# Two weight sums on VectorE, an earlier first chunk, and plain products moved between the MLP's loops

## The chip, the core and the metric

The kernel runs on one core of a Trainium2 chip. The metric is the device time of one execution in microseconds (us); a time is given as the median of several executions. The engines are TensorE (PE, matmul, with its weight load PEld), VectorE (DVE), ScalarE (ACT), GpSimd (POOL) and SyncE (SP, which here only issues DMAs). GpSimd's queue issues DMAs too, the accumulating ones.

## The reference

A decoder trunk of two layers on 1024 tokens of 1024 features, in float32. Layer 0 mixes tokens with multi-head latent attention (MLA), layer 1 with stick-breaking attention. Each is followed by cross-attention into 256 memory tokens and an MLP with squared ReLU:

```python
for i in range(DEPTH):
    a = rmsnorm(h, norm_mix[i])
    h = h + (mla_mixer(...) if i % 2 == 0 else stick_breaking_mixer(...))
    h = h + mem_cross_attn(rmsnorm(h, norm_cross[i]), rmsnorm(mem, norm_mem[i]), ...)
    h = h + jnp.square(jax.nn.relu(rmsnorm(h, norm_mlp[i]) @ w_in)) @ w_out   # 1024 -> 4096 -> 1024
return rmsnorm(h, norm_final)
```

## The kernel before

**Tiles.** Activations lie transposed: `x[c][f]` is a 128x512 tile of features f (8 of them) and tokens of chunk c (2 chunks of 512). A product in float32 is made of three fast matmuls (`mm3`, L103 to L105): each operand is split into a high half, a cast by ScalarE (L98, L159), and a low half, what the cast left over, a subtraction by GpSimd or VectorE (L90). Tiles come from pools by tag; a tag has a fixed number of slots (`p` 6, `w` 8, `a` 32, `g` 24, `o` 8, `f` 4, `raw` 3, `tmp` 5; in PSUM `s` 3 and `acc` 3), and a new tile waits until the oldest of its tag is free. A scheduler fixes the order of the instructions on each engine from a model of their costs.

**Sublayers.** `mla` and `stick` interleave projections and attention through `weave`, and `weave` also steps a side job, `aside[0]`, in two of three turns. `cross` ends with output units `ounit(c, m)` of 12 matmuls, each added to `x[c][m]` by `add_x` (L256). After the last feature of a chunk, `ready` finishes the RMS norm of the chunk, writes 8 normed tiles (`normed`, L212) into tiles `p` and splits them into `a` tiles for the MLP.

**MLP.** Of 4096 hidden features 3584 go through a scheme of seven products in place of eight (`seven`): two token chunks, two halves of the input and two halves of the output form 2x2 blocks. On the activation side it needs B11, B21, B22 and sums T1 to T4, on the weight side A11, A12, A22 and sums S1 to S4, where S2 = S1 + A11 and S4 = S2 + A12. `win` (14 per layer, 84 matmuls each) makes hidden tiles, squares them and spills seven of them to DRAM (L1054); `wout` (17 per layer) fetches them (`fetch`, L1069) and adds into `x`. The other 512 hidden features are "plain": 8 products of 24 matmuls before the first `win`, squared by VectorE (L991) and spilled, and 16 output products of 12 matmuls (192 matmuls) at the end of the MLP. In between `quad(k)` makes the T sums, for which VectorE computes the normed tiles again (L212) and then four sums (L879).

**Weight sums.** The side job `weight_sums` forms S1 to S4 in DRAM while the attention runs: `begin` copies one block on SP's queue (L924), `add` adds another by an accumulating DMA on GpSimd's queue (L929). There are 12 blocks per sum (`S1_out31` is a block of S1 for `w_out`, group 3, half 1). A `win` then loads three A and four S blocks of weights, a `wout` likewise (L1086).

**Ends.** After layer 0's MLP the last output products feed layer 1's norm (`stagger`, `ready`); after layer 1's they go through `finish`, which norms and writes the output.

## Time and profile before

| | us |
|---|---|
| median of 3 executions | 2764.06 (2758.38 to 2767.03) |
| the profiled execution, its own time | 2767.62 |
| its span in the trace | 2765.8 |
| TensorE busy in the span | 2574.7 |
| VectorE busy | 1640.6 |
| ScalarE busy | 1298.1 |
| GpSimd busy | 1389.3 |

The trace is of one execution. The page gives totals and groups of instructions; the answers of the trace used here are of four kinds: busy time of each engine by stretch, a timeline of single instructions, groups by line of code, and DMA issues. In a timeline the bracket at the end of a row says how long the engine stood idle before that instruction, and which instruction, or DMA, released it. The stages by time: MLA to about 500 us, cross-attention to 669, layer 0's MLP to about 1350 (`win` from 745, `wout` from 1027), stick-breaking and cross-attention to about 2060, layer 1's MLP to the end.

### The profile page before, as it was taken

Reading aid. Unit: us, or ns where it says so; the run is one execution under the profiler, and the core shown is the slowest. Engines: PE = TensorE matmul, PEld = TensorE weight load, DVE = VectorE, ACT = ScalarE, POOL = GpSimd, SP = SyncE. Lnnn points to the kernel's source line nnn. Section 1 sums busy time; section 2 is a strip of 40 time slices with the busy share of each in tenths; the row PEclk is TensorE's granted clock in tenths of the full one; section 3 lists DMA queues with packets and bytes.
Section 4 is the critical chain, followed back from the end, with each engine's and each line's share of the span. In section 5 each row is a group of like instructions: output and inputs, shape, how many; then the busy total and the mean of one; then the engine's idle time right before and its main releaser. Section 6 shows DMA issues by size and latency. Waiting matters only on the chain.

```text
span 2765.8 us, 37140 instructions
## 1 busy us (share of the span) xinstructions
PE 2574.7 (93%) x12774; PEld 2138.5 (77%) x12774; DVE 1640.6 (59%) x2754; ACT 1298.1 (47%) x2558; POOL 1389.3 (50%) x1098
## 2 busy tenths in 40 slices
PE   7897988898899989999999899989998999899997
PEld 5786877786688867888888787877776888678886
DVE  6765766666834436445655757587669343364457
ACT  6674755553345445443443333344543545454432
POOL 4443454633744439665432333436337544397653
PEclk9998999999899999999999999999999999999998
DMA  3528594510366648663251827855102655486632
GB/s 117 194 78 220 119 215 123 132 35 27 103 185 198 186 161 261 197 193 100 82 174 63 212 69 153 194 131 129 35 23 85 197 188 189 147 273 193 195 107 76
DMA packets 204206, 398.34 MB, mean 144 GB/s; under 512 B 23025, under 2 KB 77297, under 8 KB 190705
## 3 DMA queue, kind: packets, MB, share of 16 engines
q1 hardware_dynamic: 191584, 337.11, 38.8%
q0 software_dynamic: 12288, 58.73, 11.2%
q8 instruction: 100, 1.64, 0.2%
q14 instruction: 90, 0.73, 0.1%
q10 hardware_dynamic: 144, 0.13, 0.0%
HBM read 336.11 MB, written 177.21 MB: 186 GB/s over the span
## 4 chain that ended last, share of the span: by engine, by line
PE 64%; DVE 13%; DMA 4%; issue 2%; POOL 2%; ACT 2%; SPq 0%; DVEq 0%; POOLq 0%; ACTq 0%
PE ps_acc L103 13%; PE ps_acc L104 13%; PE ps_acc L105 13%; PE ps_s L103 7%; PE ps_s L104 7%; PE ps_s L105 7%; DVE p L212 2%; DVE f L462 2%; PE ps_s L398 1%; DVE p L879 1%; DVE x L256 1%; DVE p L467 1%; POOL w L90 1%; PE ps_pt L420 1%; DMA raw<-in_w_xv 1%
## 5 line engine op out<-in xcount | busy, mean ns | idle before, releaser
L90 POOL TENSOR_TENSOR w<-raw,w 128x512 fp32r<-128x512 f32 (+3 forms) x313 | 415.1, 1341 | 478.0 <-ACT w L98 338.5
L90 POOL TENSOR_TENSOR g<-tmp,g 128x512 fp32r<-128x512 f32 x176 | 238.1, 1354 | 278.5 <-ACT g L193 211.1
L103 PE MATMUL ps_acc<-a,w 128*128 128x512 f32 (+1 forms) x820 | 319.4, 390 | 14.0 <-ACT a L159 4.2
L104 PE MATMUL ps_acc<-a,w 128*128 128x512 f32 (+1 forms) x820 | 316.6, 387 | 3.8 <-DVE a L201 2.0
L105 PE MATMUL ps_acc<-a,w 128*128 128x512 f32 (+1 forms) x820 | 316.8, 386 | 2.3 <-POOL w L90 2.3
L256 DVE TENSOR_TENSOR x<-ps_acc,x 128x512 f32<-128x512 f32 x296 | 200.1, 684 | 104.8 <-PE ps_acc L105 103.0
L98 ACT CAST w<-raw 128x512 fp32r<-128x512 f32 (+2 forms) x189 | 114.2, 605 | 238.3 <-PE ps_acc L104 149.8
L103 PE MATMUL ps_s<-a,w 128*128 128x512 f32 (+1 forms) x416 | 169.1, 406 | 37.7 <-ACT a L159 21.5
L103 PEld LDWEIGHTS ps_acc<-a,w 128*128 128x128 f32 x820 | 156.5, 191 | 47.0 <-ACT a L159 4.7
L90 POOL TENSOR_TENSOR a<-p,a 128x512 fp32r<-128x512 f32 x100 | 137.0, 1375 | 102.7 <-ACT a L159 81.9
L104 PEld LDWEIGHTS ps_acc<-a,w 128*128 128x128 f32 x820 | 156.3, 191 | 36.5 <-DVE a L201 4.2
L105 PEld LDWEIGHTS ps_acc<-a,w 128*128 128x128 f32 x820 | 156.0, 190 | 33.8 <-POOL w L90 3.5
L398 PE MATMUL ps_s<-g 128*128 128x512 f32 (+3 forms) x576 | 141.1, 359 | 36.0 <-POOL g L90 29.5
L104 PE MATMUL ps_s<-a,w 128*128 128x512 f32 (+1 forms) x416 | 168.6, 405 | 5.5 <-POOL a L90 2.3
L105 PE MATMUL ps_s<-a,w 128*128 128x512 f32 (+1 forms) x416 | 166.9, 402 | 4.5 <-POOL w L90 4.5
L90 DVE TENSOR_TENSOR a<-tmp,a 128x512 fp32r<-128x512 f32 x92 | 90.9, 993 | 134.2 <-ACT a L159 133.3
L90 DVE TENSOR_TENSOR pt<-ps_pt,pt 128x512 fp32r<-128x512 f32 (+1 forms) x192 | 122.2, 639 | 67.8 <-ACT pt L176 67.1
L176 ACT CAST pt<-ps_pt 128x512 fp32r<-128x512 f32 (+1 forms) x192 | 104.9, 554 | 87.8 <-PE ps_pt L420 46.0
L103 PE MATMUL ps_acc<-o,w 128*128 128x512 f32 x304 | 129.1, 425 | 11.5 <-DVE x L256 8.5
L398 PEld LDWEIGHTS ps_s<-g 128*128 128x128 f32 x576 | 95.6, 192 | 51.3 <-POOL g L90 30.7
L159 ACT CAST a<-tmp 128x512 fp32r<-128x512 f32 x100 | 62.1, 621 | 148.6 <-DMA tmp<-B 139.1
L159 ACT CAST a<-p 128x512 fp32r<-128x512 f32 x116 | 72.0, 620 | 116.7 <-PE ps_s L104 43.0
(313 smaller groups left out, 7569.3 us busy)
## 6 DMA issues: line engine op xcount, KB each, us to landing
p<-S_in SPq DMA_DIRECT2D x112, 256.0 KB, 3.0
tmp<-T SPq DMA_DIRECT2D x112, 256.0 KB, 3.4
raw<-in_w_in SPq DMA_DIRECT2D x100, 256.0 KB, 2.9
S_in<-in_w_in POOLq DMA_DIRECT2D x24, 1024.0 KB, 10.8
S_out<-in_w_out POOLq DMA_DIRECT2D x48, 512.0 KB, 9.3
tmp<-B SPq DMA_DIRECT2D x84, 256.0 KB, 3.2
T<-tmp SPq DMA_DIRECT2D x56, 256.0 KB, 3.1
S_in<-in_w_in SPq DMA_DIRECT2D x12, 1024.0 KB, 8.9
```

What stands on the lines that cost most here:

```text
L90: eng.tensor_tensor(out=l, in0=full, in1=h.bitcast(F32), op=ALU.subtract)
L98: nc.scalar.copy(out=h, in_=raw)
L103: nc.tensor.matmul(out=ps, lhsT=wh, rhs=xh, start=start, stop=False, skip_group_check=True)
L104: nc.tensor.matmul(out=ps, lhsT=wh, rhs=xl, start=False, stop=False, skip_group_check=True)
L105: nc.tensor.matmul(out=ps, lhsT=wl, rhs=xh, start=False, stop=stop, skip_group_check=True)
L159: nc.scalar.copy(out=h, in_=src)
L176: nc.scalar.copy(out=h, in_=ps)
L212: nc.vector.scalar_tensor_tensor(out=t, in0=x[c][f], scalar=gains[:, gcol + f:gcol + f + 1], in1=rms[c][1], op0=ALU.mult, op1=ALU.mult)
L256: nc.vector.tensor_tensor(out=x[c][f], in0=ps, in1=x[c][f], op=ALU.add)
L398: nc.tensor.matmul(out=ps[:, :n], lhsT=lh, rhs=rh, start=(i == 0), stop=(i == len(passes) - 1), skip_group_check=True)
L420: nc.tensor.transpose(out=tp[:, o0:o0 + P], in_=col(probs[qi][kb // 4], kb % 4), identity=ident)
L462: nc.vector.tensor_tensor_scan(out=rev, data0=rev, data1=pt[j][:, :n], op0=ALU.mult, op1=ALU.bypass, initial=1.0 if j == len(pieces) - 1 e ...
```

## The change

1. Only S1 and S3 are formed in DRAM; the side job is stepped in one of three turns. S2 and S4 are formed by VectorE in `seven_weights`, S4 in the tile of S2, in each `win` and `wout`.
2. In `cross` all remaining output units of chunk 0 go before those of chunk 1.
3. `ready` keeps the normed tiles (tags `g` for chunk 0, `o` and `p` for chunk 1), and `quad` uses them in place. The plain input products run chunk 0 first, then chunk 1 with a `quad` before each. Their squares go to ScalarE. One T4 split in two goes to VectorE.
4. Of the plain output products' 4 hidden tiles, 2 (layer 0) or 1 (layer 1) are multiplied early, between the last `win` and the first `wout`: their operands are loaded and split during the last `win`. Each `x` tile takes one more addition for it. The rest stays at the end.

GpSimd in MLA, before: the S1 adds (L929) and the subtractions of low halves (L90; `g` for attention scores, `w` for weights).

```order
L929 DMA S1_out10_0_1306<-in_w_out 32x2x2048
L929 DMA S1_out11_0_1369<-in_w_out 32x2x2048
L929 DMA S1_in20_0_1390<-in_w_in 32x4x2048
L90 TENSOR_TENSOR g_2561<-tmp_2559,g_2560 128x512
L929 DMA S1_out20_0_1431<-in_w_out 32x2x2048
L929 DMA S1_out21_0_1463<-in_w_out 32x2x2048
L90 TENSOR_TENSOR w_2794<-raw_2791,w_2793 128x512
L90 TENSOR_TENSOR g_2663<-tmp_2661,g_2662 128x512
L929 DMA S1_in30_0_1522<-in_w_in 32x2x2048
L929 DMA S1_out30_0_1542<-in_w_out 128x2x256
L929 DMA S1_out31_0_1576<-in_w_out 128x2x256
```

And now, the end of the same sum:

```order
L90 TENSOR_TENSOR g_4310<-tmp_4308,g_4309 128x512
L929 DMA S1_in30_0_2006<-in_w_in 32x2x2048
L90 TENSOR_TENSOR g_4424<-tmp_4422,g_4423 128x512
L929 DMA S1_out30_0_2131<-in_w_out 128x2x256
L90 TENSOR_TENSOR w_4580<-raw_4577,w_4579 128x512
L90 TENSOR_TENSOR g_4469<-tmp_4467,g_4468 128x512
L929 DMA S1_out31_0_2210<-in_w_out 128x2x256
L90 TENSOR_TENSOR w_4586<-raw_4583,w_4585 128x512
L90 TENSOR_TENSOR w_4614<-raw_4611,w_4613 128x256
L90 TENSOR_TENSOR g_4552<-tmp_4550,g_4551 128x512
L90 TENSOR_TENSOR w_4620<-raw_4617,w_4619 128x384
```

The last adds of S1 stand apart, with subtractions between them. S2's adds and copies are not in the program any more.

VectorE at the entry of layer 0's MLP, before: normed tiles again (L212), T sums (L879) and squares (L991).

```order
L879 TENSOR_TENSOR p<-p 128x512
L212 SCALAR_TENSOR_TENSOR p<-x,gains,tmp 128x512
L879 TENSOR_TENSOR p<-p 128x512 x4
L212 SCALAR_TENSOR_TENSOR p<-x,gains,tmp 128x512 x2
L879 TENSOR_TENSOR p<-p 128x512
L991 TENSOR_TENSOR pt<-pt 128x512 x2
L879 TENSOR_TENSOR p<-p 128x512
L212 SCALAR_TENSOR_TENSOR p<-x,gains,tmp 128x512
L879 TENSOR_TENSOR p<-p 128x512
L212 SCALAR_TENSOR_TENSOR p<-x,gains,tmp 128x512 x2
L991 TENSOR_TENSOR pt<-pt 128x512
```

And now, from chunk 1's normed tiles on (`g` are chunk 0's kept tiles, `o` and `p` chunk 1's):

```order
L212 SCALAR_TENSOR_TENSOR o<-x,gains,tmp 128x512 x3
L212 SCALAR_TENSOR_TENSOR p<-x,gains,tmp 128x512
L212 SCALAR_TENSOR_TENSOR o<-x,gains,tmp 128x512 x3
L212 SCALAR_TENSOR_TENSOR p<-x,gains,tmp 128x512
L879 TENSOR_TENSOR g<-g,o 128x512 x3
L90 TENSOR_TENSOR a<-o,a 128x512
L879 TENSOR_TENSOR g<-g,p 128x512
L90 TENSOR_TENSOR a<-p,a 128x512
L90 TENSOR_TENSOR a<-o,a 128x512
L879 TENSOR_TENSOR o<-o 128x512
L90 TENSOR_TENSOR a<-p,a 128x512
L879 TENSOR_TENSOR o<-o 128x512 x2
```

The second computation of the normed tiles and the squares are gone from VectorE; splits of chunk 1 (L90) stand among the sums.

TensorE from the last `win` (`ps_acc<-a,a`) to the first `wout` (`ps_s<-a,w`) of layer 0, before:

```order
L105 MATMUL ps_acc_10218<-a_7576,a_10209 128x512
L103 MATMUL ps_acc_10218<-a_7582,a_10208 128x512
L104 MATMUL ps_acc_10218<-a_7583,a_10208 128x512
L105 MATMUL ps_acc_10218<-a_7582,a_10209 128x512
L103 MATMUL ps_s_10422<-a_10340,w_10382 128x512
L104 MATMUL ps_s_10422<-a_10341,w_10382 128x512
L105 MATMUL ps_s_10422<-a_10340,w_10383 128x512
L103 MATMUL ps_s_10423<-g_10346,w_10388 128x512
```

Now, at the end of the last `win`, where early plain products (`ps_acc_10266`) follow:

```order
L105 MATMUL ps_acc_10100<-a_7504,a_10091 128x512
L103 MATMUL ps_acc_10100<-a_7510,a_10090 128x512
L104 MATMUL ps_acc_10100<-a_7511,a_10090 128x512
L105 MATMUL ps_acc_10100<-a_7510,a_10091 128x512
L104 MATMUL ps_acc_10266<-a_10163,w_10142 128x512
L105 MATMUL ps_acc_10266<-a_10162,w_10143 128x512
L103 MATMUL ps_acc_10266<-a_10168,w_10142 128x512
L104 MATMUL ps_acc_10266<-a_10169,w_10142 128x512
```

and 71 matmuls behind that last `win` product, the first `wout` (`ps_s_10483`):

```order
L105 MATMUL ps_s_10384<-a_10116,w_10365 128x512
L103 MATMUL ps_s_10384<-a_10122,w_10364 128x512
L104 MATMUL ps_s_10384<-a_10123,w_10364 128x512
L105 MATMUL ps_s_10384<-a_10122,w_10365 128x512
L103 MATMUL ps_s_10483<-a_10402,w_10447 128x512
L104 MATMUL ps_s_10483<-a_10403,w_10447 128x512
L105 MATMUL ps_s_10483<-a_10402,w_10448 128x512
L103 MATMUL ps_acc_10392<-a_10162,w_10364 128x512
```

The early plain products (96 matmuls in layer 0, some of them ahead of the last `win`'s end) fill the place where the two loops met.

The diff, cut to its core:

```diff
@@ ready
-                    t = T("p")
+                    t = T("g" if c == 0 else "o" if k % 4 < 3 else "p")
                     normed(t, c, k, gcol)
-                    act[c].append(split(t, "a", nc.vector if k % 2 else nc.gpsimd))
+                    act[c].append((t, *split(t, "a", nc.vector if k % 2 else nc.gpsimd)))
@@ weave
-            if turn[0] % 3 < 2:
+            if turn[0] % 3 == 0:
                 next(aside[0], None)
@@ cross
+        for m in range(4, FT):
+            run(ounit(0, m))
         for m in range(FT):
-            if m + 4 < FT:
-                run(ounit(0, m + 4))
             run(ounit(1, m))
@@ weight_sums
         yield from add("S1", 1, 1)
-        yield from begin("S2", other("S1"))
         yield from add("S3", 1, 0)
-        yield from add("S2", 0, 0)
-        yield from begin("S4", other("S2"))
-        yield from add("S4", 0, 1)
+
+    def seven_weights(load, n, stage, tags):
...
+        a11, s1, s2 = load("A11", "raw"), load("S1", stage), T(stage)[:, :n * P]
+        take_split("A11", a11)
+        tt(nc.vector, s2, s1, a11, ALU.add)
+        take_split("S2", s2)
+        a12 = load("A12", "raw")
+        take_split("A12", a12)
+        tt(nc.vector, s2, s2, a12, ALU.add)
+        take_split("S3", load("S3", stage))
+        take_split("S1", s1)
+        take_split("A22", load("A22", "raw"))
+        take_split("S4", s2)
+        return r
@@ mlp
         def quad(k):
-            b11, b12, b22, b21 = (T("p") for _ in range(4))
-            for t, c, f in ((b11, 0, k), (b12, 1, k), (b22, 1, k + 4), (b21, 0, k + 4)):
-                normed(t, c, f, gcol)
+            b11, b12, b22, b21 = n0[k][0], n1[k][0], n1[k + 4][0], n0[k + 4][0]
...
+            b["T4"].append(split(b21, "o", ve if k % 2 else po))
+            b["T2"].append(split(b22, "g", po))
...
+        for c, ac in enumerate((a0, a1)):
+            for f in range(nk):
+                if c == 0:
+                    ws.append([load_w(ins["w_in"][i, f, j], "wwfp"[f]) for j in range(2)])
+                else:
+                    quad(f)
...
-                nc.vector.tensor_tensor(out=t, in0=t, in1=t, op=ALU.mult)
+                nc.scalar.activation(out=t, in_=t, func=AF.Square)
...
+        early, late = (range(2), range(2, nk)) if gnext is not None else (range(1), range(1, nk))
...
         for n, kp in enumerate(pairs):
-            win(n, kp)
+            win(n, kp, aside if kp == pairs[-1] else ())
+        for m in range(0, FT, 2):
+            if len(wp) <= m // 2:
+                block()
+            wh, wl = wp[m // 2]
+            for j in range(2):
+                for c in range(NC_):
+                    ps = PS("acc" if c else "s")
+                    project([(col(wh, j, ne * P), col(wl, j, ne * P))], ne, [g[c, k] for k in early], ps)
+                    add_x(c, m + j, ps)
...
-            project([w], nk, [g[c, k] for k in range(nk)], ps)
+            project([w], nl, [g[c, k] for k in late], ps)
```

## Rows read from the trace of the kernel before

**Rows 1.** the page's part 1: engine, busy time (share of the span), instructions

```profile
PE 2574.7 (93%) x12774; PEld 2138.5 (77%) x12774; DVE 1640.6 (59%) x2754; ACT 1298.1 (47%) x2558; POOL 1389.3 (50%) x1098
```

**Rows 2.** busy us by stretch: engines (instructions), granted clock, DMA share, GB/s

```profile
core 0: us, PE busy (x) PEld busy (x) DVE busy (x) ACT busy (x) POOL busy (x), PEclk, DMA share, GB/s
655.00:762.00 107.00, 87.04 (x333) 66.43 (x333) 87.15 (x104) 42.33 (x73) 73.64 (x48) 0.87 0.26 83
762.00:1010.00 248.00, 248.00 (x1074) 201.50 (x1073) 93.80 (x115) 121.00 (x203) 113.29 (x86) 1.00 0.58 180
1010.00:1060.00 50.00, 38.77 (x148) 28.51 (x147) 28.64 (x35) 27.67 (x56) 32.50 (x30) 0.90 0.76 245
1060.00:1300.00 240.00, 238.39 (x1031) 193.12 (x1030) 116.08 (x145) 98.53 (x176) 166.80 (x132) 1.00 0.61 181
1300.00:1352.00 52.00, 52.00 (x229) 42.36 (x229) 38.03 (x49) 25.86 (x45) 31.74 (x25) 1.00 0.22 65
2045.00:2155.00 110.00, 90.32 (x349) 68.68 (x348) 88.25 (x104) 44.38 (x76) 75.42 (x49) 0.89 0.28 89
2400.00:2450.00 50.00, 37.94 (x147) 27.88 (x146) 29.42 (x35) 26.82 (x55) 32.33 (x30) 0.90 0.74 244
2690.00:2766.00 76.00, 55.37 (x337) 48.65 (x335) 61.62 (x134) 18.14 (x37) 26.34 (x20) 0.88 0.23 78
```

**Rows 3.** timeline of TensorE in MLA: start, length, instruction, [idle before, releaser]

```profile
258.94 0.80 PE L398 MATMUL ps_s<-g 128*128 128x512 f32 x1 [15.35 <-POOL g L90]
...
420.38 0.80 PE L398 MATMUL ps_s<-g 128*128 128x512 f32 x1 [10.86 <-POOL g L90]
```

**Rows 4.** timeline of GpSimd in MLA, the two adds before those waits

```profile
254.29 1.15 POOL L929 DMA_DIRECT2D S_out<-in_w_out  x1 [12.76 <-DMA S_out<-S_out]
...
415.99 1.16 POOL L929 DMA_DIRECT2D S_out<-in_w_out  x1 [17.03 <-DMA S_in<-S_in]
```

**Rows 5.** DMA issues, 210 to 260 us: count, KB each, us to landing

```profile
S_out<-in_w_out POOLq DMA_DIRECT2D x5, 512.0 KB, 18.7
```

**Rows 6.** the page's DMA issues, whole program, same columns

```profile
S_out<-in_w_out POOLq DMA_DIRECT2D x48, 512.0 KB, 9.3
```

**Rows 7.** timeline of VectorE at the first MLP's entry, first and last

```profile
669.87 6.10 DVE L212 SCALAR_TENSOR_TENSOR p<-x,gains,tmp 128x512 f32<-128x512 f32 x6 [0.76 <-ACT tmp L115]
...
741.80 1.75 DVE L879 TENSOR_TENSOR p<-p 128x512 f32<-128x512 f32 x1
```

**Rows 8.** timelines of TensorE and of SP from last win to first wout

```profile
1018.49 0.39 PE L105 MATMUL ps_acc<-a 128*128 128x512 f32 x1
1027.45 0.80 PE L103 MATMUL ps_s<-a,w 128*128 128x512 f32 x1 [8.57 <-ACT a L159]
...
1023.77 0.45 SPq L1069 DMA_DIRECT2D tmp<-B  x1
```

**Rows 9.** VectorE's groups, 655 to 762 us: busy us, mean ns, idle

```profile
L212 DVE SCALAR_TENSOR_TENSOR p<-x,gains,tmp 128x512 f32<-128x512 f32 x32 | 37.0, 1192 | 1.1 <-ACT tmp L115 1.1
L879 DVE TENSOR_TENSOR p<-p 128x512 f32<-128x512 f32 x16 | 20.2, 1270 | 0.1
L991 DVE TENSOR_TENSOR pt<-pt 128x512 f32<-128x512 f32 x8 | 9.4, 1186 | 6.1 <-ACT pt L990 6.1
```

**Rows 10.** GpSimd's groups, 655 to 762 us, same columns

```profile
L90 POOL TENSOR_TENSOR g<-p,g 128x512 fp32r<-128x512 f32 x12 | 21.8, 1829 | 7.6 <-ACT g L159 7.6
L90 POOL TENSOR_TENSOR a<-p,a 128x512 fp32r<-128x512 f32 x13 | 19.9, 1544 | 14.6 <-ACT a L159 14.6
```

**Rows 11.** VectorE's groups of the whole program, each shape apart

```profile
L256 DVE TENSOR_TENSOR x<-ps_acc,x 128x512 f32<-128x512 f32 x296 | 200.1, 684 | 104.8 <-PE ps_acc L105 103.0
```

**Rows 12.** timeline of VectorE, one addition without and one beside GpSimd

```profile
1005.80 0.69 DVE L879 TENSOR_TENSOR f<-tmp,pt 128x512 f32<-128x512 f32 x1 [0.77 <-ACT pt L1016]
...
716.40 1.77 DVE L879 TENSOR_TENSOR p<-p 128x512 f32<-128x512 f32 x1
```

More of the change, by code (lines that the diff above doesn't have):

```diff
@@ L934, in blk @@
             return lambda *key: block(*key, *rk)
-        def other(name):
-            return lambda *key: whole(name, *key)
         yield from begin("S1", blk(1, 0))
@@ L961, in mlp @@
         gcol = G_MLP + 8 * i
-        (a0, _, _), (a1, _, _) = take(0), take(1)
+        n0, n1 = take(0)[0], take(1)[0]
+        a0, a1 = ([t[1:] for t in n] for n in (n0, n1))
         nk = FPART // P
@@ L1041, in e7, with also @@
                 square(u2)
-            seven(wa, b, 4, ("s", "acc")[n % 2], (e1, e2, e3, e4, e5, e6, e7))
+            evict = [e1, e2, e3, e4, e5, e6, e7]
+            for j, f in enumerate(aside):
+                def also(ps, e=evict[j], f=f):
+                    e(ps)
+                    f()
+                evict[j] = also
+            seven(wa, b, 4, ("s", "acc")[n % 2], evict)
             g21, g12, g22 = p1, u2, u3
@@ L1056, in mlp, with plain, block @@
         pairs = list(range(len(PAIRS)))
-        for n, kp in enumerate(pairs):
-            win(n, kp)
+        def plain(cf, tag):
+            for c, k in cf:
+                t = T("tmp")
+                nc.sync.dma_start(out=t, in_=kept[c, k])
+                g[c, k] = split(t, tag, ve if k % 2 else po)
+        early, late = (range(2), range(2, nk)) if gnext is not None else (range(1), range(1, nk))
+        ne, nl = len(early), len(late)
+        g, wp = {}, []
+        def block():
+            raw = T("raw")[:, :2 * ne * P]
+            for j in range(2):
+                nc.sync.dma_start(out=col(raw, j, ne * P), in_=ins["w_out"][i, 0, 2 * len(wp) + j][:, :ne * P])
+            wp.append(split(raw, "w", po))
+        aside = [lambda: plain([(0, k) for k in early], "a"), block, lambda: plain([(1, k) for k in early], "a"), block]
+        for n, kp in enumerate(pairs):
+            win(n, kp, aside if kp == pairs[-1] else ())
[3 more added lines that the diff above has]
+            wh, wl = wp[m // 2]
+            for j in range(2):
+                for c in range(NC_):
+                    ps = PS("acc" if c else "s")
+                    project([(col(wh, j, ne * P), col(wl, j, ne * P))], ne, [g[c, k] for k in early], ps)
+                    add_x(c, m + j, ps)
         ready_b = {}
@@ L1073, in wout, with load @@
             m = 2 * mp
[L1075 to L1078 removed]
+            def load(name, tag):
+                t, j = T(tag), 0
                 while j < len(win_):
@@ L1118, in mlp @@
                         tt(ve, t_, t_, p1[mp], op)
-        g = {}
-        for c in range(NC_):
-            for f in range(nk):
-                t = T("tmp")
-                nc.sync.dma_start(out=t, in_=kept[c, f])
-                g[c, f] = split(t, "a", nc.vector if f % 2 else nc.gpsimd)
+        plain([(c, k) for c in range(NC_) for k in late], "a")
         def ounit(c, m, w):
             ps = PS("acc" if m % 2 else "s")
-            project([w], nk, [g[c, k] for k in range(nk)], ps)
+            project([w], nl, [g[c, k] for k in late], ps)
             add_x(c, m, ps, gnext)
         def load(b, tags=("w", "f")):
-            return load_w(ins["w_out"][i, 0, b], tags[b % len(tags)])
+            return load_w(ins["w_out"][i, 0, b][:, ne * P:], tags[b % len(tags)])
         if gnext is None:
@@ L1142, in prod @@
                         ws.append(load(m, ("w", "f", "p", "w", "f", "p", "w", "p")))
-                    gs = (g[c, k] for k in range(nk))
-                    project([ws[m]], nk, [(h[:, cols], l[:, cols]) for h, l in gs], ps)
+                    gs = (g[c, k] for k in late)
+                    project([ws[m]], nl, [(h[:, cols], l[:, cols]) for h, l in gs], ps)
                 finish(c, cols, prod, engs)
```

35 lines of the change are left out of this document (15 added, 20 removed).

## The prediction

> **What bounds the kernel now.** I read the engine totals first. TensorE is busy 2574.7 of 2765.8 us and no other engine passes 60% [rows 1], so only stretches in which TensorE stands still, or runs at the lower clock, can be won back. The stretches of the span show where they are. In the first-layer `win` blocks it is busy in all 248.00 us and issues 1074 matmuls, 4.33 per us [rows 2]; that is the steady rate against which I measure the others. Four kinds of stretch fall short:
>
> - MLA, near 259 and 420 us: TensorE waits 15.35 and 10.86 us, each time for a low half `g` that GpSimd subtracts [rows 3]. GpSimd itself stood 12.76 and 17.03 us at the issue of an accumulating DMA (L929) before it got to those subtractions [rows 4]. The shortage is in the transfers: from 210 to 260 us an add takes 18.7 us to land [rows 5], against 9.3 over the program [rows 6].
> - The entry of each MLP, 655 to 762 and 2045 to 2155 us: 333 and 349 matmuls where the steady rate gives 463 and 476. That is 30.1 and 29.4 us lost, with the granted clock at 0.87 and 0.89 [rows 2]. VectorE is the late engine: its run starts at 669.87 and ends with the subtraction at 741.80 [rows 7].
> - From the last `win` to the first `wout`, 1010 to 1060 and 2400 to 2450: 148 and 147 matmuls for 216.5, so 15.8 and 16.0 us lost [rows 2]. TensorE waits 8.57 us because SP fetches the first tile at 1023.77, behind the last stores [rows 8].
> - The ends of the MLPs, where VectorE works 38.03 of 52.00 us beside a full TensorE, and 61.62 of 76.00 us [rows 2].
>
> The matmuls themselves stay: the same products in another order.
>
> **The change part by part.**
>
> *Weight sums in MLA, +25 us.* S2 and S4 no longer go through DRAM: of 48 copies and 48 adds per layer, 24 of each are left, issued in one third of the turns rather than two thirds. The order shows what that does on GpSimd: before, eight S1 adds stand with three subtractions between them; in the new kernel three adds stand among eight subtractions, and the S2 copies that shared the transfers are gone. An add waits for the add eight before it, so what decides is the spacing of eight adds against their landing time. Before, the landing time (18.7 us) was doubled by the crowd; now eight adds spread over at least twice the time with half the traffic beside them. Of the 26.2 us of TensorE's two waits [rows 3] I take 22 back, and 3 for the slow clock behind them (its first matmul of 512 columns there takes 0.80 us). The bounds are 8 (the last S1 and S3 add still wait, and only part of the crowd goes) and 32 (both waits and 6 of clock).
>
> *Less transfer elsewhere, +3 us.* The cross and stick-breaking stages lose adds too; bounds 0 and 12. Which waits there are the transfers' I can't tell, so I take little.
>
> *Entries, +13 us each, 26.* VectorE's 74 us are 32 normed tiles (L212, 37.0; 16 of them made a second time for the T sums), 16 sums (20.2), 8 squares (9.4) and the rest splits [rows 9]. Kept tiles halve L212 (-18.5), the squares go to ScalarE (-9.4; ScalarE is busy 42.33 of 107 [rows 2] and takes 8 more instructions), two T4 splits come on (+2). VectorE falls by 26 to 48 us, against 192 plain matmuls / 4.33 = 44.3 us of TensorE: level. Chunk 0 also leaves cross-attention with 8 units (96 matmuls, 22 us) of chunk 1 behind it instead of 5 (14 us), which covers most of its norm chain and its 8 tiles. What is late next is GpSimd: in the second half of the plain products it has 14 T splits at 1.83 and 4 splits at 1.54 [rows 10] and three weight splits of the first `win` that I price alike, 36 us beside 22 us of TensorE, and T2, the second product's operand, comes last. I charge 10 us for that, 4 us for the start of chunk 0 and 3 for the clock: 17 of 30 stay lost. Bounds 5 (VectorE or GpSimd binds as before) and 28.
>
> *Early plain products, +12 and +8 us.* 96 matmuls (22 us) in layer 0 and 48 (11 us) in layer 1 move between the last `win` and the first `wout`. In the order, 71 of the 96 stand behind the last matmul of the last `win`: 71 / 4.33 = 16.4 us of cover against the 8.96 us from the end of the `win` (1018.49) to the first `wout` matmul [rows 8]; their operands are queued on SP ahead of the last block's stores. Of 15.8 us I take 12, since the ramp of the second `wout` stays. In layer 1 the cover is half, and each early product is 3 matmuls (0.69 us) with an eviction of 0.684 [rows 11], so VectorE paces it: 8. Bounds together 10 and 30. The 16 added evictions per layer, 11 us of VectorE, are hidden there only as long as TensorE would wait anyway.
>
> *Ends, -5 and -2 us.* The late products shrink by the same 22 and 11 us while VectorE's evictions and norms stay. In layer 0 the 38.03 us of VectorE [rows 2] now stand beside less TensorE work, so part of the early gain is given back. Bounds 0 and -18 together.
>
> *Sums on VectorE, -4 us.* 2 sums x (14 `win` + 17 `wout`) x 2 layers = 124. An SBUF addition takes 0.69 us alone and 1.77 beside GpSimd [rows 12]; at 1.1 us it is 2.2 us per block in stretches where VectorE is busy 93.80 of 248.00 and 116.08 of 240.00 us [rows 2], so it lies beside other work. Queued behind a sum on VectorE are the evictions on which TensorE's PSUM tiles depend, and S4 is formed in S2's tile, so it waits until GpSimd has subtracted S2. With three PSUM tiles of each kind a wait under one product (12 matmuls, 2.8 us) is covered. Without that cover a sum costs its full 0.69 us. I take -4, bounds 0 and -15. A gain in the blocks is excluded: they are full.
>
> The Trainium skill (SBUF — State Buffer, "Who interferes with whom") says that a VectorE instruction with two SBUF inputs contends with a GpSimd instruction that reads SBUF for one shared port, an exclusive lock whose loser fully blocks. The trace agrees as far as 0.69 against 1.77 us goes, and the rule speaks against this change: all 124 sums have two SBUF inputs and run beside GpSimd's subtractions. By it with nothing hidden the term would be 124 x 1.77 = 219 us; by the row of the busy shares it is hidden.
>
> **Sum.** 25 + 3 + 26 + 20 - 7 - 4 = 63 us. The profiled execution took 2767.6 us, so 2704.6 there. It lies 3.5 us above the median of the runs shown (2764.1), so the predicted time is **2701 us**.
>
> **The rivals.**
>
> - *The adds still wait.* The last S1 and S3 adds still wait for the add eight before. For it: each add still carries that wait in the order. Against it: the spacing. MLA gives 8 instead of 25: 2718 us.
> - *GpSimd takes VectorE's place.* At the entries GpSimd, busy 73.64 of 107 us already [rows 2], leaves 5 us of gain each (16 less), and the ends cost 18 instead of 7: 2701 + 16 + 11 = 2728 us. For it: T2 comes last and is wanted second. Against it: its splits should be shorter beside a calmer VectorE.
> - *More is won.* If VectorE's 26 us come off the entries in full (26 more) and MLA gives its 32 (7 more): the sum is then 96 and the time 2668 us.
> - *Slower side: the sums hold the evictions.* Place: VectorE in `win` and `wout`. A sum waits in order for its DMA, or S4 for GpSimd, and the evictions stand behind it. If each of 124 sums delays TensorE by 0.69 us, that is 85.6 in place of 4: 2783 us. It eats the whole gain at a mean delay of (63 + 4) / 124 = 0.54 us, and passes 0.3% slower at 0.61 us. Against it: VectorE has over half its time free there.
> - *The port lock of the skill's rule*, with each sum exposed at its contended 1.77 us: 219 in place of 4, so 2916 us. The four additions that end each `win` already have two SBUF inputs beside a busy GpSimd, and TensorE is full there [rows 2], so it gets little.
>
> That the change doesn't do what it says I exclude: the order shows the recomputation gone, and the early products ahead of the first `wout`.
>
> **How the numbers follow.** Chances: forecast 0.52 (own range 2678 to 2722), adds still wait 0.12, GpSimd binds 0.15, more is won 0.13, sums hold evictions 0.07, port lock 0.01. The range reaches from the case of more down to 2662 to the far side of GpSimd's case, 2736; it leaves out the two slow cases and the tails of those two, some 0.18. About 0.3% (8 us) is what a measurement of this kernel can tell from no change. Slower by more: the port lock, and the sums' case at over 0.61 us, 0.05 together. Within: the sums' case near 0.55 us, 0.03. Faster: the rest, 0.92.
>
> **What would show it.** MLA: no wait of TensorE over 5 us for `g`, GpSimd's waits at L929 under 10 us in sum, adds that land within 12 us near 220 us. Entries: VectorE's run from the first L212 to the last L879 under 55 us, L212 32 times in the program instead of 64; if TensorE's longest wait in the first `win` is for GpSimd's `g`, GpSimd is the new bound. Exits: no 8 us gap, over 195 matmuls in the 50 us around the join in layer 0. Sums: TensorE's matmuls per us in the `win` and `wout` stretches stay at 4.33 and 4.30; if they fall by 2% or more while VectorE's additions wait for ScalarE, GpSimd or a DMA, the slow rival is true. The prediction is wrong if the blocks lose what the joins win, or if the entries stay above 25 us of loss each.

## The result and the profile after

| | before | after |
|---|---|---|
| median | 2762.9 us (4 runs) | 2678.6 us (2677.2 to 2681.7, 4 runs) |
| ratio | | 0.9697 (95%: 0.9679 to 0.9715) |
| profiled execution, its span | 2767.6, 2765.8 | 2677.2, 2675.4 |

The forecast was 2701 us, 2662 to 2736. The time lies inside, and 84 us were won where 63 were forecast. That single number hides errors of both signs, which the traces show.

The page after: the engine totals, TensorE's scores (`L398`, the group with GpSimd's `g`), and VectorE's evictions.

```profile
PE 2543.8 (95%) x12750; PEld 2119.5 (79%) x12750; DVE 1729.9 (65%) x2866; ACT 1308.4 (49%) x2582; POOL 1365.0 (51%) x1054
...
L256 DVE TENSOR_TENSOR x<-ps_acc,x 128x512 f32<-128x512 f32 x312 | 211.8, 684 | 98.9 <-PE ps_acc L105 96.6
...
L398 PE MATMUL ps_s<-g 128*128 128x512 f32 (+3 forms) x576 | 137.9, 354 | 3.2 <-ACT p L459 1.7
```

VectorE is 89 us busier and TensorE's busy time has gone down by 31 us: fewer matmuls ran at the lower clock (the mean granted clock is 0.984 after 0.97). TensorE's idle time before all the scores' matmuls together is 3.2 us, 1.7 of it for ScalarE's `p`, where the two waits of [rows 3] alone were 26.

Busy time by stretch after, laid on the same stages as [rows 2] (us, each engine with its instructions, granted clock, DMA share, GB/s); the first is the MLA stretch in which those two waits lay.

```profile
core 0: us, PE busy (x) PEld busy (x) DVE busy (x) ACT busy (x) POOL busy (x), PEclk, DMA share, GB/s
200.00:400.00 200.00, 199.29 (x1171) 174.10 (x1170) 145.41 (x339) 135.66 (x304) 83.44 (x73) 1.00 0.43 100
606.00:712.00 106.00, 89.42 (x360) 70.83 (x359) 64.35 (x80) 48.73 (x85) 72.41 (x47) 0.92 0.23 75
712.00:956.00 244.00, 243.62 (x1054) 197.50 (x1053) 118.15 (x137) 120.08 (x201) 116.65 (x89) 1.00 0.50 164
956.00:1006.00 50.00, 47.98 (x206) 37.95 (x206) 40.43 (x56) 26.69 (x55) 30.56 (x29) 1.00 0.67 216
1040.00:1240.00 200.00, 200.00 (x867) 162.61 (x866) 106.92 (x133) 80.12 (x138) 134.08 (x103) 1.00 0.48 143
1986.00:2092.00 106.00, 95.41 (x391) 75.96 (x390) 54.14 (x70) 51.07 (x89) 69.05 (x45) 0.93 0.31 100
2600.00:2675.40 75.40, 49.92 (x284) 42.21 (x282) 61.37 (x139) 17.54 (x39) 24.87 (x22) 0.83 0.23 76
```

MLA is full. The `win` stretch has 1054 matmuls in 244 us, 4.32 per us, and the `wout` stretch 867 in 200, 4.34: the sums cost nothing there. The join in layer 0 has 206 matmuls in 50 us instead of 148. The entries are better (TensorE is busy 84 and 90% of them); with the end of the program (66%) they are still the worst stretches.

**Where the time went.** Both kernels have the same products (48 matmuls of 256 columns have become 24 of 512), so I count in each trace how much of TensorE's work has been issued (each matmul at its steady interval: 0.228 us at 512 columns, 0.119 at 256) and read by how much the new kernel is ahead at equal work. The difference over a stage is what the stage won, in the two profiled executions. That of the kernel before was 5 us longer than its median, so the stages add up to more than the 84 us that the medians show:

| stage | forecast | read |
|---|---|---|
| MLA and cross-attention, layer 0 | 25 and part of 3 | 51.3 |
| entry of the MLP, layer 0 | 13 | 7.4 |
| `win` stretch | part of -4 | 0.2 |
| join of `win` and `wout`, layer 0 | 12 | 8.7 |
| end of the MLP, layer 0 | -5 | -4.8 |
| stick-breaking and cross-attention, layer 1 | part of 3 | 21.4 |
| entry, layer 1 | 13 | 8.0 |
| join, layer 1 | 8 | 4.4 |
| end, layer 1 | -2 | -6.2 |
| sum | 63 | 90.4 |

The attention stages gave 73 instead of 28; entries, joins and ends together gave 17 where I had 39. In the tables and below, "ahead" or "behind" at equal work is always read in this way, in single executions.

### The profile page after: what moved, and what is told of

It reads as the page before. It is cut to its first block, busy times and chain, and to the rows that moved or that the text cites. A ratio compares the mean times of both kernels' runs of the same rounds, so it can differ in the third digit from the quotient of the medians.

```text
span 2675.4 us, 36846 instructions
## 1 busy us (share of the span) xinstructions
PE 2543.8 (95%) x12750; PEld 2119.5 (79%) x12750; DVE 1729.9 (65%) x2866; ACT 1308.4 (49%) x2582; POOL 1365.0 (51%) x1054
## 5 line engine op out<-in xcount | busy, mean ns | idle before, releaser
L90 POOL TENSOR_TENSOR w<-raw,w 128x512 fp32r<-128x512 f32 (+3 forms) x309 | 408.8, 1328 | 470.7 <-ACT w L98 327.0
L90 POOL TENSOR_TENSOR g<-tmp,g 128x512 fp32r<-128x512 f32 x176 | 237.0, 1348 | 289.2 <-ACT g L193 214.5
L103 PE MATMUL ps_acc<-a,w 128*128 128x512 f32 (+1 forms) x801 | 311.4, 389 | 9.9 <-DVE tmp L377 4.7
L104 PE MATMUL ps_acc<-a,w 128*128 128x512 f32 (+1 forms) x801 | 309.7, 387 | 11.2 <-DVE a L90 9.1
L105 PE MATMUL ps_acc<-a,w 128*128 128x512 f32 (+1 forms) x801 | 308.9, 386 | 0.9 <-POOL w L90 0.9
L256 DVE TENSOR_TENSOR x<-ps_acc,x 128x512 f32<-128x512 f32 x312 | 211.8, 684 | 98.9 <-PE ps_acc L105 96.6
L98 ACT CAST w<-raw 128x512 fp32r<-128x512 f32 (+2 forms) x177 | 105.6, 598 | 166.7 <-PE ps_acc L104 108.3
L104 PEld LDWEIGHTS ps_acc<-a,w 128*128 128x128 f32 x801 | 152.1, 190 | 43.3 <-DVE a L90 9.9
L103 PEld LDWEIGHTS ps_acc<-a,w 128*128 128x128 f32 x801 | 152.3, 190 | 42.7 <-DVE tmp L377 5.4
L105 PEld LDWEIGHTS ps_acc<-a,w 128*128 128x128 f32 x801 | 152.2, 190 | 31.2 <-POOL w L90 1.6
L104 PE MATMUL ps_s<-a,w 128*128 128x512 f32 (+1 forms) x386 | 153.7, 398 | 15.3 <-DVE a L90 11.7
L103 PE MATMUL ps_s<-a,w 128*128 128x512 f32 (+1 forms) x386 | 151.9, 397 | 13.3 <-ACT w L98 7.3
L90 DVE TENSOR_TENSOR pt<-ps_pt,pt 128x512 fp32r<-128x512 f32 (+1 forms) x192 | 122.5, 641 | 52.1 <-ACT pt L176 50.8
L90 POOL TENSOR_TENSOR a<-p,a 128x512 fp32r<-128x512 f32 x84 | 110.2, 1317 | 82.6 <-ACT a L159 72.4
L105 PE MATMUL ps_s<-a,w 128*128 128x512 f32 (+1 forms) x386 | 151.8, 394 | 0.2 <-POOL w L90 0.2
L90 DVE TENSOR_TENSOR a<-tmp,a 128x512 fp32r<-128x512 f32 x92 | 88.6, 965 | 81.2 <-ACT a L159 80.7
L398 PE MATMUL ps_s<-g 128*128 128x512 f32 (+3 forms) x576 | 137.9, 354 | 3.2 <-ACT p L459 1.7
L159 ACT CAST w<-raw 128x512 fp32r<-128x512 f32 (+3 forms) x132 | 75.7, 574 | 119.4 <-PE ps_acc L104 46.1
L103 PE MATMUL ps_acc<-o,w 128*128 128x512 f32 x288 | 121.2, 421 | 7.4 <-DVE x L256 7.1
L879 DVE TENSOR_TENSOR p<-p,raw 128x512 f32<-128x512 f32 x56 | 59.3, 1069 | 97.1 <-POOL w L90 70.9
```

Of the source, the lines that this page charges most:

```text
L90: eng.tensor_tensor(out=l, in0=full, in1=h.bitcast(F32), op=ALU.subtract)
L98: nc.scalar.copy(out=h, in_=raw)
L103: nc.tensor.matmul(out=ps, lhsT=wh, rhs=xh, start=start, stop=False, skip_group_check=True)
L104: nc.tensor.matmul(out=ps, lhsT=wh, rhs=xl, start=False, stop=False, skip_group_check=True)
L105: nc.tensor.matmul(out=ps, lhsT=wl, rhs=xh, start=False, stop=stop, skip_group_check=True)
L159: nc.scalar.copy(out=h, in_=src)
```

## The experiments

All ratios are to the kernel before, run on the same chip; 1 - ratio times 2760 us is the gain. Differences to the new kernel are differences of medians, partly taken on different chips; by the ratios they come out up to 5 us different.

**Each part undone in the new kernel.** First the sums: S2 and S4 in DRAM again.

```diff
-            if turn[0] % 3 == 0:
+            if turn[0] % 3 < 2:
...
         yield from add("S1", 1, 1)
+        yield from begin("S2", other("S1"))
         yield from add("S3", 1, 0)
+        yield from add("S2", 0, 0)
+        yield from begin("S4", other("S2"))
+        yield from add("S4", 0, 1)
...
+            r[name] = split(load(name, "raw" if name[0] == "A" else stage), tag, nc.gpsimd)
```

> The changed kernel with its first part undone: S2 and S4 formed in DRAM again, the side job in two of three turns. Read at equal shares of TensorE's work, the changed kernel has won 51 us by the end of layer 0's cross-attention and 21 more in the stick-breaking stages, where I had forecast 25 + 3. Theory: nearly all of that is the sums' traffic, so 2679 + 60 to 75 = 2739 to 2754 us, with TensorE's waits of over 10 us for g back in MLA. Rival: the forecast's 28 us was right for the traffic and the rest of the attention's gain comes from other instructions standing elsewhere in the order: about 2707 us.

Measured: 2723.4 us, 0.9865 (0.9842 to 0.9887), 45 us slower than the new kernel. The waits of MLA are back; TensorE's timeline in this run:

```profile
261.70 0.79 PE L398 MATMUL ps_s<-g 128*128 128x512 f32 x1 [15.83 <-POOL g L90]
...
418.57 0.79 PE L398 MATMUL ps_s<-g 128*128 128x512 f32 x1 [5.61 <-POOL g L90]
```

At equal work it is 2 us ahead of before at the end of layer 0's cross-attention, where the new kernel is 51 ahead. So all of the gain up to there is this part's. The theory's 60 to 75 us is too much nevertheless: this kernel keeps more at the joins (at equal work it wins 13 us at the first, the new one 9). TensorE has no wait over 1.71 us there in this run. In the new kernel, where VectorE makes the sums, TensorE waits for an eviction on VectorE soon after the first `wout`:

```profile
1020.50 0.47 PE L103 MATMUL ps_s<-a,p 128*128 128x512 f32 x1 [2.64 <-DVE x L879]
```

Second, the alternating output units of cross-attention, with the weight tiles that they had:

```diff
-                    wo[m] = load_w(ins["w_xo"][i, m], ("w", "w", "f", "w", "w", "f", "p", "p")[m])
+                    wo[m] = load_w(ins["w_xo"][i, m], ("w", "w", "f")[m % 3])
...
-        for m in range(4, FT):
-            run(ounit(0, m))
         for m in range(FT):
+            if m + 4 < FT:
+                run(ounit(0, m + 4))
             run(ounit(1, m))
```

> The changed kernel with the output units of the two chunks alternating again. Theory: chunk 0's norm chain is then covered by 5 instead of 8 units, 8 us less in each layer, of which half is seen: 2683 to 2690 us. Rival: the chain of chunk 1 ends at the same time either way, and it is what the first win waits for: 2679 us.

Measured: 2680.0 us, 0.9718 (0.9702 to 0.9733): 1 us from the new kernel by the medians, 6 by the ratios, whose intervals overlap. The earlier first chunk is worth nothing that can be told from none, which is the rival's case.

Third, the entry of the MLP as before (kept tiles, order of the plain products, squares, and the T4 splits all on GpSimd):

```diff
-                    t = T("g" if c == 0 else "o" if k % 4 < 3 else "p")
+                    t = T("p")
...
+            b11, b12, b22, b21 = (T("p") for _ in range(4))
+            for t, c, f in ((b11, 0, k), (b12, 1, k), (b22, 1, k + 4), (b21, 0, k + 4)):
+                normed(t, c, f, gcol)
...
+                nc.vector.tensor_tensor(out=t, in0=t, in1=t, op=ALU.mult)
```

> The changed kernel with the entry of the MLP as before: normed tiles computed twice, plain products alternating over the chunks, squares on VectorE. The two entries won 7.4 and 8.0 us. Theory: VectorE's run there goes back from under 55 to about 74 us and the entries lose those 15 us and some more, since the earlier chunk 0 no longer helps: 2693 to 2705 us. Rival: the norm chains set the entry and not VectorE's amount of work: within 5 us of 2679.

Measured: 2706.4 us, 0.9811 (0.9796 to 0.9826), 28 us slower. The entry stretch of layer 0 in this run:

```profile
606.00:730.00 124.00, 101.58 (x395) 78.20 (x394) 96.71 (x115) 49.34 (x84) 80.11 (x51) 0.88 0.22 72
```

VectorE is busy 97 of 124 us there instead of 64 of 106. At equal work the entries are 2 and 5 us behind the kernel before: with sums on VectorE the old entry is worse than it was. The first `win`'s sums stand in the same queue, which would explain it; that they are the cause was not shown. The new entry is thus worth 7.4 and 8.0 against before, and about 10 and 13 beside the sums.

Fourth, all plain output products at the end:

```diff
-        early, late = (range(2), range(2, nk)) if gnext is not None else (range(1), range(1, nk))
+        early, late = range(0), range(nk)
...
-            win(n, kp, aside if kp == pairs[-1] else ())
+            win(n, kp)
```

> The changed kernel with all plain output products at the end of the MLP. The joins of win and wout won 8.5 and 4.5 us and the ends gave back about 5 and 6. Theory: the early products are worth little in sum, 2 to 6 us: 2681 to 2685 us, with the waits of 8 us at the joins back. Rival (the forecast): 20 won and 7 given back, so 2692 us.

Measured: 2703.2 us, 0.9801 (0.9784 to 0.9818), 25 us slower; theory and rival both said less. TensorE's first `wout` matmul in this run:

```profile
968.99 0.79 PE L103 MATMUL ps_s<-a,w 128*128 128x512 f32 x1 [8.69 <-ACT a L159]
```

The wait is that of [rows 8], but the ramp behind it is worse: at equal work the joins lose 8 and 7 us against before. So a join with sums on VectorE costs some 8 us more, and the early products cover that too. And the end of layer 0, where the new kernel gives back 4.8 us, seems to be no loss in the end: its next stages win 21.4, those of this kernel, which gives nothing back, 16.

**The sums alone, in the kernel before.** The diff is the first part of the change and nothing else (`seven_weights`, S1 and S3 only in `weight_sums`, one turn in three).

> The kernel before with the first part alone: S1 and S3 formed in DRAM in one of three turns, S2 and S4 on VectorE. Undone in the changed kernel it was worth 45 us, while the changed kernel's MLA alone won 51. Theory: the traffic is worth 50 to 60 us in the attention stages, and the sums cost some 8 us at each join of win and wout, where the first wout now waits for a chain of two sums: 2759 - 40 = 2714 to 2724 us, with the joins of this kernel more than 5 us later than those of before. Rival (the forecast's terms): 28 won and 4 lost, 2735 us.

Measured: 2728.0 us, 0.9877 (0.9857 to 0.9897), 32 us faster than before. By stage at equal work, in the profiled executions: 49 us won by the end of layer 0's cross-attention and 13 in layer 1's stages, 3 lost at each entry, 7 and 9 at the joins. So the two sums' way through DRAM was worth some 62 us, and VectorE's sums cost about 22 here, at entries and joins alone. Together that is 40 us, the difference of the two profiled executions; the medians show 32, so single stages are known to some 8 us. The total lies between theory and rival; the parts are the theory's, with a cost at the entries that it lacked. The first wait at the join itself is no longer than before, 8.61 us; the loss is in the ramp behind it.

**Density or amount.**

```diff
-            if turn[0] % 3 == 0:
+            if turn[0] % 3 < 2:
                 next(aside[0], None)
```

> The changed kernel with the side job stepped in two of three turns, as before: half the copies and adds, at the old density. Theory: the amount of traffic in flight is what held the adds, since the S2 copies and S4 copies ran beside them; without them a dense issue does little harm: 2679 to 2688 us. Rival: the density of the adds on GpSimd's queue, each waiting for the add eight before, is what held GpSimd: a wait of over 5 us at L929 is back in MLA and 15 to 30 us with it, 2694 to 2709 us.

Measured: 2678.7 us, 0.9703 (0.9682 to 0.9724), the same as the new kernel. GpSimd's waits at the adds in this run (us in total, times, longest):

```profile
POOL S_out L929 <- issue: 7.7, 2, 4.0
POOL S_out L929 <- PE ps_acc L105: 7.3, 1, 7.3
```

Some waiting is back; TensorE waits 3.32 us for `g` once in MLA. At equal work this run is 6 us behind the new kernel at the end of layer 0's cross-attention and makes up 4 of them in layer 1. In the new kernel no add waits, and the landing times of all its adds are:

```profile
L929 POOL DMA_DIRECT2D S_out<-in_w_out x32: 820/996/1189, 295.6 to 1840.1; - x32
...
its engine sat idle before it (us, times) until:
...
DMA to landing us min/median/max: 4.3/7.2/10.6
```

18.7 us, the median of [rows 5], became 10.6 at most. With half the amount in flight an add lands sooner, however closely the adds are issued.

What an add waits for is another matter, and the forecast had it wrong. In the kernel before, the stop of 12.76 us in [rows 4] came right behind the add issued at 240.38 us, and the stop of 17.03 us right behind the one at 397.82:

```profile
L929 POOL DMA_DIRECT2D S_out<-in_w_out x1: 1153/1153/1153, 240.4 to 240.4; - x1
...
DMA to landing us min/median/max: 13.6/13.6/13.6
...
L929 POOL DMA_DIRECT2D S_out<-in_w_out x1: 1139/1139/1139, 397.8 to 397.8; - x1
...
DMA to landing us min/median/max: 17.8/17.8/17.8
```

Both times GpSimd went on 0.33 us after that landing (at 253.96 and 415.66), while the add eight before had landed long ago, at 225.43 and 374.75. These are the two adds of shape 128x2x256 that end each sum. In all 13 stops at this place (kernel before, sums in DRAM again, this run) the second of the pair starts 0.33 or 0.34 us after the first has landed, and in no trace does it start earlier. Of the 80 adds of other shapes in the kernel before, 65 start while the one ahead of them is still under way. So it is the spacing of this pair that counted, against one landing time. In the new kernel's MLA the first lands in 4.7 and 4.5 us and the second follows 8 and 22 us behind it, so nothing stops. Here the two stand close again, and the stops are short (7.34 and 3.64 us) because the first lands in 8.5 and 4.5. Density brings the stop, the amount in flight makes it long. Why the second add waits for the first was not tried. The stop of 6.65 us just ahead of 240.38, before the first of the pair, is of another kind: it ended 0.36 us after the fourth add back had landed.

**Are the sums hidden?** S2's addition three times in every block:

```diff
-        tt(nc.vector, s2, s1, a11, ALU.add)
+        for _ in range(3):
+            tt(nc.vector, s2, s1, a11, ALU.add)
```

> The changed kernel with the addition S2 = S1 + A11 carried out three times in every block, so 124 more additions of the same form on VectorE. Theory: the sums are hidden beside TensorE in the win and wout blocks, so only those at the two joins show, 2 x 1.4 us: 2679 to 2685 us. Rival (the slow rival of the forecast): evictions queue behind them and each costs its 0.69 us, 2679 + 86 = 2765 us.

Measured: 2713.9 us, 0.9831 (0.9811 to 0.9851): 35 us for 124 more additions, 0.28 us each. Between the two theories, and the stretches say why (`win`, then `wout`):

```profile
717.00:961.00 244.00, 242.54 (x1050) 197.05 (x1049) 138.46 (x159) 117.49 (x200) 117.96 (x87) 1.00 0.49 160
1045.00:1245.00 200.00, 190.63 (x801) 153.34 (x802) 126.92 (x143) 75.00 (x131) 136.95 (x98) 0.97 0.48 142
```

In `win` the rate holds (1050 against 1054 in 244 us); in `wout` it falls from 867 to 801 in 200 us. VectorE's and then TensorE's timeline at one of the places:

```profile
1086.07 3.41 DVE L879 TENSOR_TENSOR f<-f,raw 128x512 f32<-128x512 f32 x2 [1.19 <-POOL p L90]
1089.41 0.68 DVE L879 TENSOR_TENSOR x<-x,ps_acc 128x512 f32<-128x512 f32 x1
...
1090.14 0.79 PE L103 MATMUL ps_acc<-o,p 128*128 128x512 f32 x1 [3.64 <-DVE x L879]
```

The sums wait for GpSimd, take 1.7 us each, an eviction stands behind them, and TensorE waits 3.64 us for that eviction. This is the mechanism of the forecast's slow rival. Inside the loops the new kernel's two sums per block stay below the point at which it begins; four in a `wout` would not.

**No sums in DRAM at all.**

```diff
+        a11, a21, a22 = load("A11", "raw"), load("A21", stage), load("A22", "raw")
...
+        tt(nc.vector, s1, a21, a22, ALU.add)
         tt(nc.vector, s2, s1, a11, ALU.add)
...
+        tt(nc.vector, a21, a11, a21, ALU.add)
...
-    aside[0] = weight_sums(0)
```

> The changed kernel with nothing formed in DRAM: S1 = A21 + A22 and S3 = A11 + A21 are formed on VectorE too, from a fourth block of weights that is loaded in place of two sums; the side job is gone. Theory: the rest of the traffic costs little in the attention stages, 0 to 8 us, and four sums per block are as hidden as two, but the first wout at each join waits for one more sum: 2672 to 2682 us. Rival: VectorE becomes late in the wout blocks, where it was busy 116 of 240 us before: TensorE's rate there falls and the time is over 2690 us.

Measured: 2715.8 us, 0.9834 (0.9812 to 0.9856), 37 us slower than the new kernel. The rival holds: `win` and `wout` stretches of this run,

```profile
712.00:956.00 244.00, 244.00 (x1057) 198.43 (x1056) 132.35 (x159) 120.07 (x201) 122.72 (x88) 1.00 0.44 149
1050.00:1250.00 200.00, 185.31 (x772) 148.07 (x771) 121.37 (x137) 71.89 (x127) 131.39 (x93) 0.97 0.41 125
```

full in `win`, 772 matmuls instead of 867 in `wout`. There TensorE waits for evictions on VectorE (1045 to 1250 us of this run), of which the new kernel has none between 1045 and 1250 us:

```profile
PE ps_acc L103 <- DVE x L879: 8.2, 3, 4.0
PE ps_s L103 <- DVE x L879: 6.3, 2, 5.7
```

**So: four sums in `win`, two in `wout`.** The sums of the edit above as a function of their own, `seven_weights4`, for `win` alone, with `weight_sums` left for `w_out`'s S1 and S3:

```diff
-            wa = seven_weights(load, 4, "p", "wwwaaaa")
+            wa = seven_weights4(load, 4, "p", "wwwaaaa")
...
-        keys = [(kind, g, h) for g in range(len(GROUPS)) for kind, h in (("in", 0), ("out", 0), ("out", 1))]
+        keys = [(kind, g, h) for g in range(len(GROUPS)) for kind, h in (("out", 0), ("out", 1))]
```

> The changed kernel with all four sums of a win formed on VectorE (S1 and S3 too, from A21 in place of the two loads) and the two of a wout as they are; only the w_out sums S1 and S3 are left in DRAM. Forming all of them on VectorE lost its 37 us in the wout stretches and none in the win stretches. Theory: the win stretches hide four sums (VectorE busy 118 of 244 us), a fifth less is loaded there, and a quarter of the first traffic goes from the attention stages: 2671 to 2678 us. Rival: the extra sum ahead of the first win at each entry is on the path and eats that: 2680 to 2686 us.

Measured: 2670.4 us, 0.9665 (0.965 to 0.9679), 8 us faster than the new kernel, as the theory had it. At equal work 2.8 us come by the end of layer 0's attention and about 4 in layer 1's.

**Is GpSimd the late engine at the entry?** In the new kernel TensorE waits at three places there, twice for a split of the first normed tiles and once at the first `win`:

```profile
625.11 0.72 PE L104 MATMUL ps_s<-a,w 128*128 128x512 f32 x1 [4.85 <-DVE a L90]
...
657.61 0.80 PE L104 MATMUL ps_acc<-a,w 128*128 128x512 f32 x1 [4.52 <-DVE a L90]
...
685.45 0.50 PE L103 MATMUL ps_s<-g,w 128*128 128x512 f32 x1 [4.14 <-ACT w L159]
```

The third, followed back on ScalarE and VectorE:

```profile
684.78 0.62 ACT L159 CAST w<-p 128x512 fp32r<-128x512 f32 x1 [0.56 <-DVE p L879]
...
681.34 1.73 DVE L90 TENSOR_TENSOR o<-g,o 128x512 fp32r<-128x512 f32 x1 [9.95 <-POOL g L90]
683.00 1.75 DVE L879 TENSOR_TENSOR p<-p,raw 128x512 f32<-128x512 f32 x1
```

The weight cast waits for the sum S2 (683.00), which stands behind a T4 split that waited 9.95 us for GpSimd. The experiment takes six T splits from GpSimd:

```diff
-            b["T4"].append(split(b21, "o", ve if k % 2 else po))
-            b["T2"].append(split(b22, "g", po))
+            b["T4"].append(split(b21, "o", ve))
+            b["T2"].append(split(b22, "g", ve))
```

> The changed kernel with the splits of T2 and T4 on VectorE: GpSimd has 8 T splits at each entry instead of 14. In the changed kernel the first win waits 4.14 us for a weight cast, which waits for the sum on VectorE, which stands in order behind a T4 split that waits 9.95 us for GpSimd. Theory: GpSimd is the late engine at the entry, as the forecast's charge had it, so 3 to 5 us come back at each: 2669 to 2673 us. Rival: the norm chain of chunk 1 and VectorE's own sums set that time, and the splits only move the load: 2677 to 2684 us.

Measured: 2670.7 us, 0.9666 (0.9652 to 0.968), 8 us faster. TensorE's third wait in this run:

```profile
685.23 0.50 PE L103 MATMUL ps_s<-g,w 128*128 128x512 f32 x1 [1.80 <-ACT w L159]
```

At equal work 5.6 us come back at layer 0's entry, so GpSimd was the late engine there. At layer 1's entry it is only 1.2 us; what sets that one stays open.

**Two early tiles in layer 1 too.**

```diff
-        early, late = (range(2), range(2, nk)) if gnext is not None else (range(1), range(1, nk))
+        early, late = (range(2), range(2, nk))
```

> The changed kernel with two of four plain tiles early in layer 1 too, 96 matmuls instead of 48 at its join. Theory: the join in layer 1 wins 4 more (8.5 as in layer 0 instead of 4.5) and the end loses about as much, since VectorE's evictions and the output norm there stay: 2677 to 2682 us. Rival: the join gains the whole difference to a steady rate and the end is bound by its last norm alone, 2670 us.

Measured: 2682.5 us, 0.9703 (0.9684 to 0.9722), no difference to the new kernel that can be told. The join wins some 7 us more at equal work, and the end loses as much more, in an execution 4 us above the run's median. TensorE's waits for the last norm on VectorE, 6.58 and 5.87 us in the new kernel (first two rows), come as one of 12.43 here, no longer in sum; what is added are waits of 4.74 and 2.81 us ahead of it:

```profile
2659.20 0.47 PE L114 MATMUL ps_pt<-ident,sm_y 128*128 128x128 f32 x1 [6.58 <-DVE sm_y L152]
2665.76 0.47 PE L114 MATMUL ps_pt<-ident,sm_y 128*128 128x128 f32 x1 [5.87 <-DVE sm_y L152]
```

```profile
2652.69 1.09 PE L139 MATMUL ps_pt<-ident,tmp 128*128 128x128 f32 x4 [4.74 <-DVE tmp L132]
2656.58 0.66 PE L139 MATMUL ps_pt<-ident,tmp 128*128 128x128 f32 x2 [2.81 <-DVE sm_i L146]
...
2675.19 0.47 PE L114 MATMUL ps_pt<-ident,sm_y 128*128 128x128 f32 x1 [12.43 <-DVE sm_y L152]
```

**Both gains together:** four sums in `win`, T2 and T4 splits on VectorE.

> The changed kernel with both edits that were each worth 8 us: all four sums of a win on VectorE, and the splits of T2 and T4 on VectorE. Theory: the first acts in the attention stages and the blocks, the second at the entries, so they add: 2660 to 2665 us. Rival: the first win's S1 and S2 now both stand on VectorE behind six more splits, so part of the second gain goes: 2666 to 2671 us.

Measured: 2662.6 us (5 runs), 0.9643 (0.9619 to 0.9666), 16 us faster than the new kernel: the gains add. It has the lowest median of all versions.

## Why the prediction was right, and where it wasn't

The direction held, because TensorE's lost time could be counted by stretch and the change removes work from the engines that were late there. That the time lies inside the range is partly luck: the attention stages gave 73 us in the profiled executions, where the upper bounds of their two terms together were 44, and entries, joins and ends, with 22 us less than forecast, made up for half of what was priced too low. Step by step:

- **Weight sums in MLA, +25 (bounds 8 and 32): too small by half; the undone and the alone run show 49 to 51, cross-attention included.** The two waits I counted gave back 17.2 and 14.5 us at equal work, 32 with the slow clock behind them, which is my upper end: there was no reason to take less, because nothing of the cause was left. The step that failed is that I stopped at the two long waits: another 20 us lay in shorter losses before, between and behind them. A third stop of GpSimd alone (7.01 us at 349.93, with a wait of 2.99 us on TensorE) gave back 4.8. "What decides is the spacing of eight adds" is wrong too: the adds that stood waited for the landing of the add right ahead. That no stop was left came true all the same, since the change sets this pair apart and shortens its landing.
- **Less transfer elsewhere, +3 (bounds 0 and 12): the largest miss for its size, with 13 us in layer 1 from the sums alone.** Of the other 8 some 5 seem handed on by the end of layer 0 (21.4 against 16 without early products); the rest is not placed. I wrote that I couldn't tell which waits were the transfers'. A cause that I couldn't place I priced near nothing, and even its upper bound was too low: the side job runs through all of both attention layers, and I looked at the 40 us around its worst waits. How the sums cost these 13 us stays open: from 1380 to 2010 us no wait of TensorE in the kernel before is over 2.8 us. Some 11 lie in one stretch, where the granted clock was 0.95 before (first row) and 0.99 with the sums alone changed (second row), for nearly the same matmuls:

```profile
1850.00:2045.00 195.00, 178.27 (x988) 151.71 (x987) 132.22 (x253) 95.45 (x209) 87.20 (x68) 0.95 0.34 81
```

```profile
1809.00:1993.00 184.00, 171.47 (x985) 146.03 (x985) 132.04 (x251) 95.36 (x210) 84.25 (x63) 0.99 0.25 63
```

- **Entries, +13 each: 7.4 and 8.0.** The charge of 4 us for the start of chunk 0 was right (4.85), but the same wait comes for chunk 1 (4.52), which I left out, since VectorE makes all eight normed tiles before the first split. GpSimd is late next, as charged, in layer 0; in layer 1 what sets the entry stays open. The earlier chunk 0, to which I gave 8 us of cover, is worth nothing that shows.
- **Early products, +12 and +8: 8.7 and 4.4 against before, yet 25 us against the new kernel without them.** I priced the join as it was before. With sums on VectorE the join is 8 us worse, and the early products pay for that first. Two parts of one change were priced each against the old kernel, and this is where they meet.
- **Ends, -5 and -2: -4.8 and -6.2.** The first seems to be handed back in the next stage; in the second TensorE waits 15.4 us for norms on VectorE over the whole program, 8.6 before.
- **Sums on VectorE, -4: 0 in the blocks, and the cost stands at entries and joins,** 22 us in the kernel with the sums alone. The slow rival (sums hold the evictions) is true as a mechanism: inside the loops it begins between two and four sums per `wout`, and then the run is 35 us longer. The port lock at 1.77 us exposed per sum is not what happened.

In the profiled executions the total is 90 us for 63: the attention stages were priced 45 us too low, the blocks 4 too low, and entries, joins and ends 22 too high. The medians' 84 us are 21 above the forecast.

## What to carry to other kernels

Where a background job fills the DMA queues, price its removal over every stage in which it runs, not at the two longest waits: the short waits were worth more than half as much again. When a change moves work onto an engine, price its other parts against the kernel with that work, since entries and joins, where that engine is late, are where it shows. And before an engine gets still more work, double it by experiment: inside the loops two sums per block were free, four were free in `win` and not in `wout`, and only the stretches told the two apart. Last, where a queue stands, look up which transfer landed just before it went on: [rows 4] name a copy both times, and it was an add.

## What the runs showed of the hardware

GpSimd can be held far longer by VectorE than the sharing in [rows 12] suggests. In the run with T2 and T4 split on VectorE, one GpSimd subtraction, 1.30 us elsewhere, spans 9.44 us in the profile, whose spans on GpSimd are rough (first row), while VectorE runs additions and subtractions with two SBUF inputs at 0.6 us from start to start throughout (the others):

```profile
662.90 9.44 POOL L90 TENSOR_TENSOR g<-o,g 128x512 fp32r<-128x512 f32 x1 [4.29 <-ACT g L159]
```

```profile
662.70 1.28 DVE L879 TENSOR_TENSOR o<-o 128x512 f32<-128x512 f32 x2
663.90 0.68 DVE L879 TENSOR_TENSOR p<-p 128x512 f32<-128x512 f32 x1
664.51 1.88 DVE L879 TENSOR_TENSOR o<-o,g 128x512 f32<-128x512 f32 x3
...
670.53 0.68 DVE L90 TENSOR_TENSOR o<-g,o 128x512 fp32r<-128x512 f32 x1
```

The new kernel has it too: a subtraction of 7.64 us at 660.70. In [rows 7] VectorE's instructions took 1.75 us beside GpSimd, so there the two seem to have taken turns. Here VectorE's kept to 0.68 us each, and GpSimd's ended 1.13 us after their row (672.34 against 671.21), as if it got in only then. The Trainium skill (SBUF — State Buffer, "Who interferes with whom") calls the shared port pair an exclusive lock, says that a VectorE instruction with two SBUF inputs contends for it with a GpSimd instruction that reads SBUF, and of VectorE's two-port modes that whoever issues first has the pair for the whole instruction, while the other fully blocks. These rows agree with the blocking, and show it lasting through a row of 14 instructions. Why the engines take turns in one place and not in the other was not tried.
